# Branch outputs: norm in two VectorE passes, other PSUM banks for the second column half, gate tiles first in their pool, weight parts at the heads' priority

## The chip, the core and the metric

One core of a Trainium2 chip runs the whole program in one launch. The metric is the device time in microseconds. The kernel before takes 2545.5 us as the median of 3 runs (2544.97 to 2547.24).

## The reference

The program is one inference step of a two-layer encoder in float32 over 640 tokens: one prompt of 512 and 8 sample sequences of 16, with the same weights. D_MODEL is 1024. Each layer computes

```
h   = rmsnorm(x, ln1);  proj = h @ w_in            # u, va, q|k|v, z, b, a, ga, gb
u   = gelu(u);  vn = layernorm(gelu(va), g, b)     # branch A
z_a = u * (tril(W_s) @ vn + b_s)                   # per group of 128 columns, chunks of 128 rows
q,k,v = silu(causal_conv(qkv));  o, S = gated_delta_rule(l2norm(q), l2norm(k), v, g, beta, S0)
z_b = rmsnorm(o, o_norm) * silu(z)                 # branch B, 8 heads
x  += (sigmoid(ga) * (z_a @ p_a) + sigmoid(gb) * (z_b @ p_b)) @ w_o
x  += relu(rmsnorm(x, ln2) @ w_up)**2 @ w_down
```

with `layernorm(x) = (x - mean) / sqrt(var + eps) * g + b` over the 1024 columns. The outputs are the final norm of x, the convolution and delta-rule states, and `vn` of the sample rows.

## The kernel before

Activations lie transposed: 128 features on the partitions, 8 chunks of features, 640 tokens along the free dimension. To keep float32 accuracy, each operand of a large matmul is the sum of two parts, hi (rounded by an ACT copy, line 131) and lo (the DVE subtraction x - hi, line 132); `split` makes both. Three matmuls per 128 features (hi·hi, hi·lo, lo·hi) stand for one. The generator `three` issues 48 matmuls of 320 columns for one weight block of 128x1024, into a pair of PSUM banks (tag `g`, two pairs). Four more banks are used one at a time, two with tag `c` and two with tag `d`.

**Weights.** `Feed` holds the fixed order of the 304 blocks (128x1024 each, 512 KB). `load` brings a block into one of three `raw` tiles through SP's queue, and `parts` splits it into `whi` and `wlo`, two buffers each. `gemm` takes the parts of its block and at once asks for those of the next, whose buffers come free when PE has finished the block before this one.

**Order of the work.** PE's order is the order in which the program is written (line 1110). For the other engines a list scheduler, run when the kernel is built, chooses by modelled durations: among the instructions whose inputs are ready in its model, the one with the lowest number goes first. The number is the place in the program, less the offset of the `high_priority` block around it. Each engine then runs its list strictly in that order, waiting on semaphores. In `parts` the offset is 1, in the pieces that `paced` hands out it is AHEAD = 200 (the delta rule's `prepare`) or 2 * AHEAD (its `chain`).

**Stages of a layer.** `heads` runs the projections of q, k, v, z and the gates as 10 slots of gemms, with `gating`, `prepare`, `chain` and `roots` of the delta rule paced between their matmuls. `gating` (lines 353 to 433) computes beta and decay from a small 128x128 weight `wb`, which it loads itself. Then `merge` (lines 923 to 1027):

- `gemm_as` (lines 248 to 265) computes va with tokens on the partitions: two halves of 512 columns, in each five accumulators (one per 128 tokens, a bank each), over four weight blocks. When a half's matmuls are all done, `va` (lines 944 to 956) takes each accumulator: gelu on ACT, `bn_stats` on DVE. After the second half it normalises the 128x1024 tile `vn`: aggregate and add eps on DVE, power -1/2 on POOL, then -mean·rate on DVE, an ACT pass, a DVE multiply by g (line 955) and a POOL add of b (line 956). Both halves use the same five banks: four of the two `g` pairs, and a `d`.
- Beside it `zb` makes z_b: per head it loads three 128x640 tiles, multiplies o by its rate on POOL (line 974), then on DVE by the norm weight and z (line 975), and splits the result into Bh and Bl.
- In the pool `sp` the p_b gemms follow (`pb`), each read out of PSUM by one DVE multiply into the tile `mix` (line 1010), with a gate tile `sg` that `gated` loads. The pool is allocated where the tiles of `zb` and the rows g and b of the norm lay, and `mix` is its first tile; a tile waits for the readers of those that it overlaps. The spatial products, the p_a gemms and w_o come after.

`mlp` follows: 32 up and 32 down blocks.

Of the kernel before, what the change touches and what calls it, by code (L numbers as in the profile page):

```python
# [9 lines left out]
F32 = mybir.dt.float32  # L10
F32R = mybir.dt.float32r
AF = mybir.ActivationFunctionType
ALU = mybir.AluOpType
# [4 lines left out]
P = 128  # L18
D = 1024
NT = 640  # L20
NP = 512
KC = 8
H = 8
DEPTH = 2
# [6 lines left out]
HT = NT // 2  # L31
# [8 lines left out]
AHEAD = 200  # L40
# [22 lines left out]
def encoder(ctx, tc, xin, wblk, wba, sct, sdelta, prow, pcol, gates, wst, bsr, convw, consts, delta0,  # L63
            y_out, conv_out, dp_out, ds_out, gv_out):
    nc = tc.nc
# [7 lines left out]
    cp = pool("const")  # L73
# [30 lines left out]
    mask64, maskb, odd = mis[:, 0:128], mis[:, 128:136], mis[:, 136:138]  # L104
    par = cp.tile([P, 2], F32, name="par")
    unit = cp.tile([P, 16], F32, name="unit")

    def load_rest():
        nc.sync.dma_start(cst[:, 1:3, :], consts[:, P:3 * P].rearrange("p (a b) -> p a b", a=2))
        nc.sync.dma_start(blk16, consts[:, 4 * P:640])  # L110
        nc.sync.dma_start(cap[:], consts[:, 640:1280].rearrange("p (a b) -> p a b", a=5))
        nc.sync.dma_start(mis[:], consts[:, 1280:1418])


        nc.vector.tensor_scalar(cap[:], cap[:], 1e26, None, op0=ALU.mult)
        nc.vector.tensor_reduce(par[:], maskb.rearrange("p (b j) -> p j b", j=2), axis=AX.X, op=ALU.add)
        nc.vector.tensor_reduce(unit[:], ident.rearrange("p (c i) -> p i c", i=16), axis=AX.X, op=ALU.add)
# [12 lines left out]
    def split(dst_hi, dst_lo, src):  # L130
        nc.scalar.activation(dst_hi, src, AF.Copy)  # L131
        nc.vector.tensor_tensor(dst_lo, src, dst_hi.bitcast(F32), op=ALU.subtract)  # L132

    class Feed:
# [13 lines left out]
        def parts(self, pl):  # L148
            raw = self.raw.pop(0)
            hi = pl.tile([P, D], F32R, tag="whi", bufs=2, name="whi")  # L150
            lo = pl.tile([P, D], F32R, tag="wlo", bufs=2, name="wlo")
            with tc.high_priority(offset=1):
                split(hi[:], lo[:], raw[:])
            return hi, lo

# [21 lines left out]
    def bank(tag, nm):  # L177
        return psp.tile([P, 512], F32, tag=tag, name=f"ps_{nm}")

    def pair(nm):  # L180
        return psp.tile([P, 2, 512], F32, tag="g", bufs=2, name=f"pg_{nm}")
# [66 lines left out]
    def gemm_as(l, b0, ah, al, nm, use):  # L248

        for n in range(2):  # L250
            g0, g1 = pair(f"{nm}{n}a"), pair(f"{nm}{n}b")
            accs = [g0[:, 0, :], g0[:, 1, :], g1[:, 0, :], g1[:, 1, :], bank("d", f"{nm}{n}")[:]]
            for j in range(4):
                w = feed.take(l, b0 + 4 * n + j)
                for t in range(5):
                    for kk in range(2):
                        k = 2 * j + kk
                        ath, atl = ah[:, k, t * P:(t + 1) * P], al[:, k, t * P:(t + 1) * P]
                        wh, wl = (v[:, kk * 512:(kk + 1) * 512] for v in w)
                        mm(accs[t], ath, wh, k == 0, False)  # L260
                        mm(accs[t], ath, wl, False, False)
                        mm(accs[t], atl, wh, False, k == KC - 1)
                yield
            for t in range(5):
                use(t, n, accs[t])
# [87 lines left out]
    def gating(l, pk, pl, out):  # L353

        whl = pl.tile([P, 2, HT], F32R, tag="sh", name=f"whl{l}")[:, 0, 0:256].rearrange("p (k c) -> p k c", k=KC)
        wb = pl.tile([P, P], F32, tag="w4", name=f"wb{l}")[:].rearrange("p (k c) -> p k c", k=KC)
        rest = pl.tile([P, 5, P], F32, tag="osb", name=f"gt{l}")[:].rearrange("p t n -> p (t n)")
        nc.sync.dma_start(wb, wba[l])
        split(whl[:, :, 0:16], whl[:, :, 16:32], wb)
        yield 15  # L360

        ps = pair(f"ba{l}")
# [15 lines left out]
        z, az, e, w, w2, p, g = (sm[:, i] for i in range(7))  # L378
# [401 lines left out]
    v2 = lambda ap: ap.rearrange("p (a n) -> p a n", a=2)  # L780
# [142 lines left out]
    def merge(l, ond, msd, gd):  # L923
        with phase(f"merge{l}", 1) as pl:
            Bh = pl.tile([P, KC, NT], F32R, name=f"Bh{l}")
            Bl = pl.tile([P, KC, NT], F32R, name=f"Bl{l}")
            with phase(f"branch{l}", 1) as po:
# [11 lines left out]
                with phase(f"ln{l}", 1, side="right") as pv, phase(f"zb{l}", 3) as pz:  # L939
                    gr = rep_row(pv, prow[l, 0:1, :], f"alg{l}", "alg")  # L940
                    br = rep_row(pv, prow[l, 1:2, :], f"alb{l}", "alb")
                    stats = [pv.tile([P, 2, 6], F32, tag="stats", bufs=5, name=f"stats{l}{t}") for t in range(5)]

                    def va(t, n, ps):
                        nc.scalar.activation(vn[:, t, n * 512:(n + 1) * 512], ps, AF.Gelu)
                        nc.vector.bn_stats(stats[t][:, n, :], vn[:, t, n * 512:(n + 1) * 512])
                        if n == 0:
                            return
                        mv = pv.tile([P, 4], F32, tag="mv", bufs=5, name=f"mv{l}{t}")
                        nc.vector.bn_aggr(mv[:, 0:2], stats[t][:].rearrange("p a b -> p (a b)"))  # L950
                        nc.vector.tensor_scalar(mv[:, 2:3], mv[:, 1:2], EPS, None, op0=ALU.add)
                        nc.gpsimd.tensor_tensor(mv[:, 3:4], mv[:, 2:3], mhalf[:, 0:1], op=ALU.pow)
                        nc.vector.scalar_tensor_tensor(mv[:, 2:3], mv[:, 0:1], -1.0, mv[:, 3:4], op0=ALU.mult, op1=ALU.mult)
                        nc.scalar.activation(vn[:, t, :], vn[:, t, :], AF.Identity, bias=mv[:, 2:3], scale=mv[:, 3:4])
                        nc.vector.tensor_tensor(vn[:, t, :], vn[:, t, :], gr[:], op=ALU.mult)
                        nc.gpsimd.tensor_tensor(vn[:, t, :], vn[:, t, :], br[:], op=ALU.add)

                    nc.scalar.activation(warm[:], phalf[:, 0:1], AF.Gelu)

                    def zb():  # L960
                        def load(m):
                            o, r, z = (pz.tile([P, NT], F32, tag=tag, name=f"{tag}{l}{m}") for tag in "orz")
                            nc.sync.dma_start(z[:], gd[3, m])
                            nc.sync.dma_start(o[:], ond[m])
                            nc.sync.dma_start(r[:], msd[1][m:m + 1, :].to_broadcast([P, NT]))
                            return o, r, z

                        tiles = [load(0), load(1)]
                        yield
                        for m in range(KC):  # L970
                            if m + 2 < KC:
                                tiles.append(load(m + 2))
                            o, r, z = tiles.pop(0)
                            nc.gpsimd.tensor_tensor(o[:], o[:], r[:], op=ALU.mult)
                            nc.vector.scalar_tensor_tensor(z[:], o[:], col[:, 40 + l:41 + l], z[:], op0=ALU.mult, op1=ALU.mult)
                            split(Bh[:, m, :], Bl[:, m, :], z[:])
                            if m:
                                yield

                    zs = zb()  # L980
                    run(gemm_as(l, WB_VA, Ah, Al, f"va{l}", va), zs)
                    run(zs)

                with phase(f"sp{l}", 1) as pq:
                    mix = pq.tile([P, KC, NT], F32, name=f"mix{l}")

                    def gated(i, m):
                        sg = pq.tile([P, NT], F32, tag="sg", bufs=3, name=f"rg{i}{l}{m}")
                        nc.sync.dma_start(sg[:], gd[i, m])
                        return sg  # L990

                    def spatial(g):
# [10 lines left out]
                        nc.gpsimd.tensor_tensor(s[:], s[:], u[:], op=ALU.mult)  # L1003
                        split(Ah[:, g, :], Al[:, g, :], s[:])

                    for g in range(KC):
                        sg = gated(1, g)

                        def pb(ps):
                            nc.vector.tensor_tensor(v2(mix[:, g, :]), ps[:, :, 0:HT], v2(sg[:]), op=ALU.mult)  # L1010

                        run(gemm(l, WB_PB + g, Bh, Bl, f"pb{l}{g}", pb))
                        for i in {3: (0, 1), 4: (2, 3), 5: (4, 5), 6: (6, 7)}.get(g, ()):
                            spatial(i)
                    nc.sync.dma_start(gv_out[l], vn[:, 4, :])
                    for m in range(KC):
                        sg = gated(2, m)

                        def pa(ps):
                            nc.vector.tensor_tensor(v2(sg[:]), ps[:, :, 0:HT], v2(sg[:]), op=ALU.mult)  # L1020
                            nc.gpsimd.tensor_tensor(mix[:, m, :], mix[:, m, :], sg[:], op=ALU.add)
                            split(Bh[:, m, :], Bl[:, m, :], mix[:, m, :])

                        run(gemm(l, WB_PA + m, Ah, Al, f"pa{l}{m}", pa))
            es = ExitStack()
# [189 lines left out]
```

## Time and profile before

| | us |
|---|---|
| median of 3 runs | 2545.5 |
| the profiled execution's own time | 2544.76 |
| its span, first to last instruction | 2543.0 |
| PE busy | 2471.5 (97%) |
| DVE busy | 1306.3 (51%) |
| ACT busy | 1011.2 (40%) |
| POOL busy | 652.6 (26%) |
| mean granted TensorE clock | 0.991 of full |

PE is the matmul engine, DVE the vector engine, ACT the scalar engine, POOL GpSimd; SP issues the DMAs. A row of the page or of a view names the source line, the engine, the operation, what it writes and reads, shapes and times. An engine's idle time is put down to the instruction whose semaphore came last. Names have their numbers shortened: `pg_va01a` is the first pair of the second column half in layer 0, `pg_va11a` the same in layer 1.

### The profile page before, as it was taken

Reading aid. Unit: us, or ns where it says so; the run is one execution under the profiler, and the core shown is the slowest. Engines: PE = TensorE matmul, PEld = TensorE weight load, DVE = VectorE, ACT = ScalarE, POOL = GpSimd, SP = SyncE. Lnnn points to the kernel's source line nnn. Section 1 sums busy time; section 2 is a strip of 40 time slices with the busy share of each in tenths; the row PEclk is TensorE's granted clock in tenths of the full one; section 3 lists DMA queues with packets and bytes.
Section 4 is the critical chain, followed back from the end, with each engine's and each line's share of the span. In section 5 each row is a group of like instructions: output and inputs, shape, how many; then the busy total and the mean of one; then the engine's idle time right before and its main releaser. Section 6 shows DMA issues by size and latency. Waiting matters only on the chain. (4 is left out here: it accounts for less than half of the span.)

```text
span 2543.0 us, 45063 instructions
## 1 busy us (share of the span) xinstructions
PE 2471.5 (97%) x18456; PEld 2392.6 (94%) x18456; DVE 1306.3 (51%) x2677; ACT 1011.2 (40%) x1952; POOL 652.6 (26%) x673
## 2 busy tenths in 40 slices
PE   7999999999999999999999999999989999999997
PEld 7899999997899999999999999999979999999997
DVE  7656677535556433333356677674274553333333
ACT  4656666533223212121346666664332222122122
POOL 3223443213422201010213343331253221011012
PEclk9999999999999999999999999999999999999998
DMA  4223433336432222222233333333554322222221
GB/s 161 90 95 101 127 94 95 115 121 229 149 116 75 67 76 76 75 76 75 81 102 108 101 99 95 95 117 117 159 201 142 96 68 76 75 76 76 77 72 66
DMA packets 124238, 261.29 MB, mean 103 GB/s; under 512 B 17232, under 2 KB 56048, under 8 KB 124032
## 3 DMA queue, kind: packets, MB, share of 16 engines
q1 hardware_dynamic: 124032, 258.41, 31.9%
q8 instruction: 145, 2.38, 0.4%
q14 instruction: 61, 0.50, 0.1%
HBM read 218.22 MB, written 40.15 MB: 102 GB/s over the span
## 5 line engine op out<-in xcount | busy, mean ns | idle before, releaser
L131 ACT ACTIVATE whi<-raw 128x1024 fp32r<-128x1024 f32 x304 | 322.1, 1060 | 1012.0 <-issue 367.7
L132 DVE TENSOR_TENSOR wlo<-raw,whi 128x1024 fp32r<-128x1024 f32 x304 | 405.1, 1332 | 161.0 <-ACT whi L131 146.6
L80 PE MATMUL pg_dn<-gl,whi 128*128 128x320 f32 x1024 | 316.6, 309 | 2.1 <-DVE gl L1085 2.1
L80 PE MATMUL pg_up<-Ah,whi 128*128 128x320 f32 x1024 | 317.1, 310 | 0.0
L80 PE MATMUL pg_dn<-gh,whi 128*128 128x320 f32 x1024 | 316.7, 309 | 0.0
L80 PE MATMUL pg_up<-Ah,wlo 128*128 128x320 f32 x1024 | 316.4, 309 | 0.0
L80 PE MATMUL pg_dn<-gh,wlo 128*128 128x320 f32 x1024 | 316.4, 309 | 0.0
L80 PE MATMUL pg_up<-Al,whi 128*128 128x320 f32 x1024 | 316.4, 309 | 0.0
L80 PE MATMUL pg_g<-Ah,whi 128*128 128x320 f32 x896 | 290.8, 325 | 0.0
L80 PE MATMUL pg_g<-Ah,wlo 128*128 128x320 f32 x896 | 278.3, 311 | 7.5 <-DVE wlo L132 7.5
L80 PE MATMUL pg_g<-Al,whi 128*128 128x320 f32 x896 | 277.7, 310 | 0.0
L1084 POOL TENSOR_TENSOR r<-r 128x640 f32<-128x640 f32 x64 | 101.8, 1590 | 684.8 <-ACT gh L1083 684.8
L80 PE MATMUL pg_p<-Ah,whi 128*128 128x320 f32 x768 | 252.1, 328 | 0.0
L80 PE MATMUL pg_p<-Ah,wlo 128*128 128x320 f32 x768 | 237.3, 309 | 0.0
L80 PE MATMUL pg_p<-Al,whi 128*128 128x320 f32 x768 | 236.8, 308 | 0.0
L80 PEld LDWEIGHTS pg_dn<-gl,whi 128*128 128x128 f32 x1024 | 192.2, 188 | 2.6 <-DVE gl L1085 2.6
L80 PEld LDWEIGHTS pg_up<-Al,whi 128*128 128x128 f32 x1024 | 192.2, 188 | 0.0
L80 PEld LDWEIGHTS pg_up<-Ah,whi 128*128 128x128 f32 x1024 | 192.2, 188 | 0.0
L80 PEld LDWEIGHTS pg_dn<-gh,whi 128*128 128x128 f32 x1024 | 192.2, 188 | 0.0
L80 PEld LDWEIGHTS pg_dn<-gh,wlo 128*128 128x128 f32 x1024 | 192.2, 188 | 0.0
L80 PEld LDWEIGHTS pg_up<-Ah,wlo 128*128 128x128 f32 x1024 | 192.2, 188 | 0.0
L80 PEld LDWEIGHTS pg_g<-Ah,wlo 128*128 128x128 f32 x896 | 169.5, 189 | 8.1 <-DVE wlo L132 8.1
(703 smaller groups left out, 5473.5 us busy)
## 6 DMA issues: line engine op xcount, KB each, us to landing
raw<-in_wblk SPq DMA_DIRECT2D x304, 512.0 KB, 3.6
gd<-sg SPq DMA_DIRECT2D x56, 320.0 KB, 2.4
rg<-gd SPq DMA_DIRECT2D x48, 320.0 KB, 2.9
S<-in_sdelta SPq DMA_DIRECT2D x16, 512.0 KB, 6.5
out<-S SPq DMA_DIRECT2D x16, 512.0 KB, 3.5
gr<-rowd SPq DMA_DIRECT2D x16, 320.0 KB, 4.9
er<-rowd SPq DMA_DIRECT2D x16, 320.0 KB, 3.2
ond<-osb SPq DMA_DIRECT2D x16, 320.0 KB, 2.2
```

What stands on the lines that cost most here:

```text
L80: nc.tensor.matmul(out, lhsT=lhsT, rhs=rhs, start=start, stop=stop, **kw)
L131: nc.scalar.activation(dst_hi, src, AF.Copy)
L132: nc.vector.tensor_tensor(dst_lo, src, dst_hi.bitcast(F32), op=ALU.subtract)
L1084: nc.gpsimd.tensor_tensor(r[:], r[:], r[:], op=ALU.mult)
```

## The change

Six edits, in the order of the file:

```diff
+    wb = cp.tile([P, P], F32, name="wb")[:].rearrange("p (k c) -> p k c", k=KC)
     def load_rest():
 ...
+        nc.sync.dma_start(wb, wba[0])
@@ Feed.parts
-            with tc.high_priority(offset=1):
+            with tc.high_priority(offset=AHEAD):
                 split(hi[:], lo[:], raw[:])
@@ gemm_as
-            g0, g1 = pair(f"{nm}{n}a"), pair(f"{nm}{n}b")
-            accs = [g0[:, 0, :], g0[:, 1, :], g1[:, 0, :], g1[:, 1, :], bank("d", f"{nm}{n}")[:]]
+            g0 = pair(f"{nm}{n}a")
+            if n == 0:
+                g1 = pair(f"{nm}{n}b")
+                accs = [g0[:, 0, :], g0[:, 1, :], g1[:, 0, :], g1[:, 1, :], bank("d", f"{nm}{n}")[:]]
+            else:
+                accs = [bank(tag, f"{nm}{n}{i}")[:] for i, tag in enumerate("ccd")] + [g0[:, 0, :], g0[:, 1, :]]
@@ gating
-        wb = pl.tile([P, P], F32, tag="w4", name=f"wb{l}")[:].rearrange("p (k c) -> p k c", k=KC)
-        nc.sync.dma_start(wb, wba[l])
         split(whl[:, :, 0:16], whl[:, :, 16:32], wb)
+        if l + 1 < DEPTH:
+            nc.sync.dma_start(wb, wba[l + 1])
@@ merge, va
-                        nc.vector.scalar_tensor_tensor(mv[:, 2:3], mv[:, 0:1], -1.0, mv[:, 3:4], op0=ALU.mult, op1=ALU.mult)
-                        nc.scalar.activation(vn[:, t, :], vn[:, t, :], AF.Identity, bias=mv[:, 2:3], scale=mv[:, 3:4])
-                        nc.vector.tensor_tensor(vn[:, t, :], vn[:, t, :], gr[:], op=ALU.mult)
-                        nc.gpsimd.tensor_tensor(vn[:, t, :], vn[:, t, :], br[:], op=ALU.add)
+                        nc.vector.scalar_tensor_tensor(vn[:, t, :], vn[:, t, :], mv[:, 0:1], gr[:], op0=ALU.subtract, op1=ALU.mult)
+                        nc.vector.scalar_tensor_tensor(vn[:, t, :], vn[:, t, :], mv[:, 3:4], br[:], op0=ALU.mult, op1=ALU.add)
@@ merge, zb
-                            nc.gpsimd.tensor_tensor(o[:], o[:], r[:], op=ALU.mult)
+                            nc.vector.tensor_tensor(o[:], o[:], r[:], op=ALU.mult)
@@ merge, pool sp
-                    mix = pq.tile([P, KC, NT], F32, name=f"mix{l}")
 ...
+                    with tc.high_priority(offset=2 * AHEAD):
+                        ahead = [gated(1, g) for g in range(2)]
+                    mix = [pq.tile([P, NT], F32, name=f"mix{l}{g}") for g in range(KC)]
                     for g in range(KC):
-                        sg = gated(1, g)
+                        sg = ahead[g] if g < 2 else gated(1, g)
 ...
-                            nc.vector.tensor_tensor(v2(mix[:, g, :]), ps[:, :, 0:HT], v2(sg[:]), op=ALU.mult)
+                            nc.vector.tensor_tensor(v2(mix[g][:]), ps[:, :, 0:HT], v2(sg[:]), op=ALU.mult)
```

In `pa` the uses of `mix[:, m, :]` become `mix[m][:]`.

## Rows read from the trace of the kernel before

**Rows 1.** Page, part 1: busy us (share of the span) and instructions.

```profile
PE 2471.5 (97%) x18456; PEld 2392.6 (94%) x18456; DVE 1306.3 (51%) x2677; ACT 1011.2 (40%) x1952; POOL 652.6 (26%) x673
```

**Rows 2.** Waits of PE: tile, releaser, total us, times, longest.

```profile
PE pg_pb L80 <- DVE mix L1010: 12.4, 2, 6.2
...
PE pg_g L80 <- DVE wlo L132: 7.5, 2, 4.0
...
PE pg_va01a L80 <- ACT vn L945: 3.4, 1, 3.4
...
PE ps_o L80 <- ACT w L662: 2.5, 10, 0.3
PE pg_va11a L80 <- ACT vn L945: 2.4, 1, 2.4
...
PE pg_ba L80 <- ACT cb L454: 1.5, 1, 1.5
```

**Rows 3.** Windows: length, busy (x instructions) by engine, clock, DMA; sum of five.

```profile
840.00:860.00 20.00, 20.00 (x139) 20.00 (x138) 7.83 (x9) 4.92 (x6) 4.03 (x3) 1.00 0.24 79
...
1848.50:1853.00 4.50, 2.08 (x10) 1.40 (x9) 4.30 (x5) 2.83 (x6) 0.95 (x1) 1.00 0.75 236
...
649.70:655.70 6.00, 6.00 (x23) 6.00 (x24) 2.34 (x2) 0.00 (x0) 1.26 (x1) 0.50 0.81 246
...
1900.30:1905.00 4.70, 4.70 (x18) 4.70 (x19) 2.40 (x2) 0.00 (x0) 1.31 (x1) 0.50 0.81 278
sum 20.30, PE 20.30 PEld 19.61 DVE 13.71 ACT 2.78 POOL 3.36; mean PE 4.06 PEld 3.92 DVE 2.74 ACT 0.56 POOL 0.67
```

**Rows 4.** Timeline of ACT, 593 to 602: start, us, instruction, idle before.

```profile
598.95 0.74 ACT L131 ACTIVATE Bh<-z 128x640 fp32r<-128x640 f32 x1 [2.67 <-DVE z L975]
599.60 0.58 ACT L945 ACTIVATE vn<-pg_va00a 128x512 f32<-128x512 f32 x1
```

**Rows 5.** Timeline of DVE in layer 0's branch stage, 592 to 652.

```profile
592.72 0.88 DVE L975 SCALAR_TENSOR_TENSOR z<-o,col,z 128x640 f32<-128x640 f32 x1 [7.11 <-POOL o L974]
...
596.77 2.15 DVE L975 SCALAR_TENSOR_TENSOR z<-o,col,z 128x640 f32<-128x640 f32 x1
...
629.72 2.36 DVE L955 TENSOR_TENSOR vn<-vn,alg 128x1024 f32<-128x1024 f32 x2 [0.85 <-ACT vn L954]
...
639.77 5.69 DVE L955 TENSOR_TENSOR vn<-vn,alg 128x1024 f32<-128x1024 f32 x3
645.39 3.35 DVE L132 TENSOR_TENSOR wlo<-raw,whi 128x1024 fp32r<-128x1024 f32 x1
648.66 1.54 DVE L1010 TENSOR_TENSOR mix<-pg_pb,rg 128x640 f32<-128x640 f32 x2
```

**Rows 6.** Timeline of SP's queue, 624 to 650.

```profile
635.84 10.45 SPq L989 DMA_DIRECT2D rg<-gd  x3
```

**Rows 7.** Groups by line, 560 to 700: busy us, mean ns, idle before.

```profile
L946 DVE BATCH_NORM_STATS2 stats<-vn 128x6 f32<-128x512 f32 x10 | 6.5, 678 | 0.2 <-ACT vn L945 0.2
...
L950 DVE BATCH_NORM_AGGREGATE mv<-stats 128x2 f32<-128x12 f32 x5 | 0.8, 187 | 0.0
...
L956 POOL TENSOR_TENSOR vn<-vn,alb 128x1024 f32<-128x1024 f32 x5 | 16.6, 3335 | 3.8 <-DVE vn L955 3.8
...
L952 POOL TENSOR_TENSOR mv<-mv,mhalf 128x1 f32<-128x1 f32 x5 | 2.7, 551 | 6.4 <-DVE mv L951 6.4
```

**Rows 8.** Timelines of ACT and of DVE in the heads stage, 106 to 120.

```profile
111.45 1.07 ACT L131 ACTIVATE whi<-raw 128x1024 fp32r<-128x1024 f32 x1
...
118.72 1.22 DVE L132 TENSOR_TENSOR wlo<-raw,whi 128x1024 fp32r<-128x1024 f32 x1
```

**Rows 9.** Timeline of SP's queue at the start of the heads, 56 to 62.

```profile
57.38 0.45 SPq L358 DMA_DIRECT2D wb<-in_wba  x1
```

**Rows 10.** One line's instructions, L662: duration min/median/max ns.

```profile
L662 ACT ACTIVATE w<-ps_w x80: 254/277/280, 171.6 to 1805.7; 128x128 f32<-128x128 f32 x80
```

**Rows 11.** Timeline of DVE at the start, 16 to 20.

```profile
17.19 1.92 DVE L132 TENSOR_TENSOR wlo<-raw,whi 128x1024 fp32r<-128x1024 f32 x1
```

More of the change, by code (lines that the diff above doesn't have):

```diff
@@ L1020, in pa @@
                             nc.vector.tensor_tensor(v2(sg[:]), ps[:, :, 0:HT], v2(sg[:]), op=ALU.mult)
-                            nc.gpsimd.tensor_tensor(mix[:, m, :], mix[:, m, :], sg[:], op=ALU.add)
-                            split(Bh[:, m, :], Bl[:, m, :], mix[:, m, :])
+                            nc.gpsimd.tensor_tensor(mix[m][:], mix[m][:], sg[:], op=ALU.add)
+                            split(Bh[:, m, :], Bl[:, m, :], mix[m][:])
                         run(gemm(l, WB_PA + m, Ah, Al, f"pa{l}{m}", pa))
```

## The prediction

> **What bounds the kernel now.** The page's first part comes first: PE is busy 2471.5 us of a span of 2543.0, DVE half of it [rows 1]. So only two things can be won: PE's idle time, and stretches in which PE runs at less than its full clock. The list of PE's waits then says where the idle time lies. The reader is to see that its largest items that this change touches belong to three places [rows 2]. The third p_b gemm of each layer waits 6.2 us for a PSUM pair that DVE has not read out (12.4). In the heads stage one gate gemm per layer waits for `wlo` (7.5). The second column half of va waits for the gelu of the first (3.4 and 2.4). Last I read windows, for the clock. After five of these six waits (all but the shortest, 2.4 us, whose window keeps 1.00) come stretches at half clock, 1.2 instead of 2.4 GHz, PE busy throughout; outside the waits themselves they sum to 20.3 us [rows 3]. At half rate they cost 10.1 us: in the window from 649.7, 23 matmuls start in 6.0 us, where 139 in 20 us is the full rate.
>
> **The change part by part.**
>
> *Other banks for the second half.* The wait of va has this form: the second half needs the pair of the first half's tiles 0 and 1; the gelu of tile 1 stands behind a split of `Bh` on ACT, and that waited 2.67 us for DVE's `z` [rows 4], which took 2.15 us beside POOL instead of 0.88 [rows 5]. With tiles 0 to 2 in banks that nobody holds, the pair is wanted 18 matmuls later, about 18 x 0.23 = 4.1 us (0.144 us a matmul of 320 columns [rows 3], times 512/320). That covers both waits: -5.8 us. If one of the three banks is held, up to all of it stays. No other bank is late next: the first p_b gemm gets the pair of tiles 2 and 3 of the first half, free long before.
>
> *Norm in two passes, gate tiles first.* Why does the p_b readout come so late? The gate loads stand 10.45 us in SP's queue [rows 6], since their tiles lie over rows that the norm reads, and on DVE the readout stands behind three multiplies (5.69 us) and a `wlo` of 3.35, both stretched by POOL's adds of 3.3 us beside them [rows 5, 7]. Two multiplies alone take 2.36. POOL's adds, the ACT passes and the small products go; the gate loads come before the matmuls need them. What is late next is DVE itself. Per tile it now has two `bn_stats` halves, of which one falls here (0.68), the aggregate and the eps add (0.19 each at most) [rows 7], and two passes. The trace has no two-input pass with a per-partition scalar of 1024 columns; the nearest row has 640 and takes 0.88, against 0.77 for a plain product of that size, and the plain product of 1024 takes 1.18 [rows 5], so I take 1.3 (bounds 1.18 and 1.41, which is 0.88 x 1024/640). Five tiles: 5 x (0.68 + 0.38 + 2.6) = 18.3; two `wlo` of 1.22 [rows 8] and the readout of 0.8 make 21.5 us. Time for it: tile 0 has its own bank now and is done 24 matmuls or 5.4 us before va ends, less 0.6 for its gelu; the third p_b gemm starts 96 x 0.144 = 13.8 after va ends; together 18.6. The 2.9 us missing are partly given back, since neighbours start about 0.1 us before the row of the one before them ends (20 to 25 of them). I take a remaining wait of 1.5 us per layer, bounds 0 (the scheduler lets the readout in) and 6.2 (as now). So -12.4 + 3.0 = -9.4. The 8 products of `zb` that move from POOL cost DVE 0.77 each, 6 us per layer, in a stretch in which DVE waits for POOL and for loads; -1 to +1, taken as 0.
>
> On SP the two gate loads now pass a weight load. If their tiles, those of `o` in `zb`, are not free by then, that load waits behind them; two further blocks are loaded already, so I take 0. One more bound of the same place comes from rows: POOL's power of 0.55 us [rows 7] now stands between the two passes of a tile. Other DVE work is there to fill it, but if none does, five times 0.55 or 2.8 us per layer are added.
>
> The Trainium skill speaks for that bound ("SBUF — State Buffer", section "Who interferes with whom"): a DVE instruction with two SBUF inputs and a GpSimd instruction that reads SBUF exclude each other, so a power would start only when the first pass is over. The multiplies and the `wlo` stretched beside POOL's adds [rows 5, 7] agree with the rule. By it the sum would be 5.5 us less, 2519.5, which lies in this case's range.
>
> *Weight parts at AHEAD.* In the heads the `wlo` that PE wants at 116 starts at 118.72, though its `whi` was begun at 111.45 [rows 8]; DVE ran small products of `prepare` in front. `prepare` has offset 200, the parts 1. At equal offset the older goes first, and `wlo` is ready at 112.5: -7.5 us, bounds 0 and -7.5. Elsewhere (mlp, p_a, w_o) `whi` already starts when its buffer comes free, so nothing moves. Three costs. In the heads a `whi` of 1.07 us can stand in front of the 0.28 us copy `w` [rows 10] for which PE already waits 2.5 us in 10 places [rows 2]: taken +1, bounds -2.5 and +8. At the start of layer 0 the second block's `wlo` (1.92 [rows 11]) goes in front of the splits of x: +1, bounds -1 and +3 (`whi` and `wlo` together). At the start of layer 1 the group's extra parts can go in front of the last splits: +0.5, bounds -1 and +2.3.
>
> *`wb` early.* One load of 0.45 us leaves SP's queue in front of the load on which the wait of `pg_ba` (1.5) hangs: -0.5, bounds 0 and -1.5 [rows 2, 9]. The second load waits on SP for the first split, which is there at once when `wb` is loaded early; what is queued behind it is weight loads of later blocks, so 0.
>
> *Clock.* With the waits the half-clock stretches go: -10.1. A remaining 1.5 us is shorter than the 2.4 that left the clock at 1.00 [rows 3]. Lower bound: half of them stay, -5.
>
> *Sum*, against the profiled execution's own 2544.76 us (its span is 2543.0; the median of the runs shown is 0.7 above): -5.8 - 9.4 - 7.5 - 0.5 - 10.1 + 1 + 1 + 0.5 = -30.8, that is 2514.0, or 2514.7 against the median. I predict 2514; this case's own range is 2505 to 2521.
>
> **The rivals.**
>
> 1. *The heads' wait stays* (chance 0.12). The scheduler's model may not see DVE as busy as it is, or `whi` is what is late: ACT has table loads and silu there. For it: `whi` itself started late. Against: it moves ahead as well. The 7.5 and about 3 of clock stay: 2525.
>
> 2. *DVE is the new bound in front of the third p_b gemm* (0.13). For it: the 21.5 us above are more than the time there is, and the norm is older in the program than the readout, so it goes first. Against: the readout's neighbours are all work that nothing stretches now. If the 6.2 us per layer stay, and the half clock after them, 6.0 and 4.7 us [rows 3] of which half is lost (5.4): -30.8 + 9.4 + 5.4, 2529.
>
> 3. *A pass of two inputs and a scalar costs twice* (0.02). As a mechanism of this kernel: ten passes per layer cost 2.4 instead of 1.3, DVE is 11 us later per layer, and the third gemm waits 12.5: some 22 us more, and 5 of clock, 2541. Against it: 0.88 for 640 columns is not twice 0.77 [rows 5]. It is what the Trainium skill says in "Vector Engine (DVE) Microarchitecture Reference", section "Points that are easy to get wrong": such an instruction with two float32 SBUF sources "halves throughput".
>
> 4. *Slower: weight parts push the delta rule's chain* (0.07). Place: the 64 steps of the 16 chains in which PE waits for `w`. Price: up to 1.07 us each, 68 us in all. It decides from 36 us on, that is 0.56 us at every step, since 31 are won. For it: PE waits there already, in ten places. Against: the chain has twice the offset, so a `whi` is in front only when it has begun, and that was so before.
>
> 5. *The change does not do what it says* (0.04): the tiles still wait for others in their pool, or waits only move by a gemm; 2540 to 2547.
>
> **How the numbers follow.** The forecast has 0.62, the rivals 0.12, 0.13, 0.02, 0.07 and 0.04. Two runs of this kernel can be told apart by about 0.2%, 5 us. Faster by more: 0.62 + 0.12 + 0.13 + 0.02 = 0.89; within: 0.04; slower: 0.07. The range of 2505 to 2529 takes in the forecast's own and the first two rivals, less the rests of each.
>
> **What would show it.** Right: the list of PE's waits has no va tile, no `pg_g` waiting for `wlo`, and the `pg_pb` item is under 4 us in all; L956 is gone, DVE's `wlo` is near 1.22 through the branch stage; the windows after these places have clock 1.00. Wrong: new rows of `pg_pb` waiting for `mix`, with two-pass rows well above 1.3 us; `ps_o` or other chain tiles high in the list; longer waits of `pg_gf` at the start of either layer. If the span falls by under 15 us although the three waits are gone, the steps are right and the gain is lost elsewhere.

## The result and the profile after

The changed kernel takes 2526.1 us (median of 4 runs, 2525.5 to 2527.3), the kernel before 2546.3 beside it: 20.2 us less, ratio 0.992 (95% interval 0.9907 to 0.993). Predicted were 2514 and a range of 2505 to 2529: the direction and this range hold, but 20.2 us came where 30.8 were forecast, and the forecast's own range, which ended at 2521, is missed. 2526.1 lies where the first two rivals stood (2525 and 2529). The profiled execution took 2525.8 with a span of 2523.8, 19.2 less than before.

Part 1 of the page after (busy us, share, instructions), against [rows 1]:

```profile
PE 2466.8 (98%) x18456; PEld 2386.9 (95%) x18456; DVE 1308.1 (52%) x2693; ACT 1020.7 (40%) x1958; POOL 585.5 (23%) x647
```

POOL loses 67 us, and DVE, which took this work over, gains only 1.8. The two passes and the product come to 38.7 us, but the 16.6 of the multiplies by g are now inside the passes, and `wlo`, `Bl` and `z` together take 15.0 less over the span; the `z` of 2.15 us beside POOL [rows 5], for example, is gone, no `z` of that stage is above 0.89. The waits of PE after (tile, releaser, total us, times, longest), against [rows 2]:

```profile
...
PE ps_ms L80 <- ACT kg L511: 8.5, 12, 0.7
PE pg_pb L80 <- DVE mix L1015: 6.3, 2, 3.2
...
PE ps_va L80 <- DVE wlo L134: 1.8, 2, 0.9
```

The heads' waits for `wlo` and the waits of `pg_va01a` and `pg_va11a` are gone. The third p_b gemm still waits, half as long: 6.3 in all, where under 4 was the sign of being right. New are 0.9 us per layer for the `wlo` of the second weight block of va's second half. And `ps_ms`, a tile of the delta rule's `roots`, now waits twelve times 0.7 us for the ACT copy `kg`; before it did so twice (1.4 us).

PE executes the same 18456 matmuls in the same order in both programs, so each can be laid beside its twin. The table gives by how much the start of the twin moves within each stage (after minus before, us); what follows a wait at half clock has its own column.

| stage | waits, layer 0 | layer 1 | half clock | predicted |
|---|---|---|---|---|
| start of the layer | +1.8 | 0 | in the waits | +1, +0.5 |
| `pg_ba` (`wb` early) | -1.6 | 0 | 0 | -0.5 |
| heads, `pg_g` for `wlo` | -4.2 | -3.7 | -1.5, -1.4 | -7.5 |
| heads, slots 2 to 9 | +3.1 | +2.9 | 0 | +1 |
| va, second half | -3.5 +1.0 | -2.6 | -1.6, 0 | -5.8 |
| third p_b gemm | -2.9 | -3.0 | 0, -2.1 | -9.4 |

Half clock is -6.6 in all (predicted -10.1), and the columns sum to -19.3.

Windows of the kernel after (length, busy by engine, clock, DMA), against [rows 3]: the start of va's second half, and the third p_b gemm of layers 0 and 1.

```profile
594.30:600.30 6.00, 6.00 (x28) 4.95 (x28) 4.84 (x8) 2.13 (x5) 0.00 (x0) 1.00 0.93 292
640.30:646.30 6.00, 6.00 (x23) 6.00 (x24) 0.57 (x1) 0.00 (x0) 0.00 (x0) 0.52 0.79 284
...
1883.20:1889.20 6.00, 6.00 (x41) 6.00 (x42) 0.54 (x1) 0.00 (x0) 0.00 (x0) 1.00 0.89 284
```

After 3.1 us without a matmul the clock in layer 0 is half, with the same 23 matmuls in 6.0 us as before. In layer 1 it stays at 1.00 after 3.2 us.

The new wait first. Groups of ACT's table loads over the whole span, before and then after (L463/L469 are the silu of q, k and v, L812/L818 the activation of the gates):

```profile
L463 ACT ACT_TABLE_LOAD x32 | 41.1, 1283 | 0.5
...
L812 ACT ACT_TABLE_LOAD x22 | 28.2, 1283 | 0.4
```

```profile
L469 ACT ACT_TABLE_LOAD x34 | 43.6, 1283 | 0.6
L818 ACT ACT_TABLE_LOAD x34 | 43.6, 1283 | 2.2 <-DMA gd<-sg 1.6
```

Over all lines the loads rise from 79 to 95. ACT's timeline after, of one slot, shows why:

```profile
290.86 1.07 ACT L133 ACTIVATE whi<-raw 128x1024 fp32r<-128x1024 f32 x1
291.95 1.28 ACT L818 ACT_TABLE_LOAD   x1
293.24 0.70 ACT L818 ACTIVATE sg<-pg_g 128x640 f32<-128x640 f32 x1
...
294.13 1.28 ACT L469 ACT_TABLE_LOAD   x1
295.42 0.63 ACT L469 ACTIVATE vT<-yb 128x512 f32<-128x512 f32 x1
...
302.53 1.28 ACT L818 ACT_TABLE_LOAD   x1
303.82 0.71 ACT L818 ACTIVATE sg<-pg_g 128x640 f32<-128x640 f32 x1
...
306.37 0.59 ACT L511 ACTIVATE kg<-ps_kt04a 128x512 f32<-128x512 f32 x1
```

A slot holds two gate reads (`sg`, sigmoid) and one silu of v. Before, the silu came first and both gate reads shared one load. Now the first gate read comes in front of the silu, and the second needs a load of its own. These 1.28 us stand in front of `kg`, and until `kg` is copied out `ps_ms` can't have the bank that it wants.

The branch stage of layer 0 after, DVE, against [rows 5], and SP's queue, against [rows 6]:

```profile
619.76 1.28 DVE L952 BATCH_NORM_STATS2 stats<-vn 128x6 f32<-128x512 f32 x2
...
630.85 1.29 DVE L960 SCALAR_TENSOR_TENSOR vn<-vn,mv,alb 128x1024 f32<-128x1024 f32 x1 [0.24 <-POOL mv L958]
632.05 1.22 DVE L134 TENSOR_TENSOR wlo<-raw,whi 128x1024 fp32r<-128x1024 f32 x1
...
635.70 2.47 DVE L960 SCALAR_TENSOR_TENSOR vn<-vn,mv,alb 128x1024 f32<-128x1024 f32 x2
638.18 1.22 DVE L134 TENSOR_TENSOR wlo<-raw,whi 128x1024 fp32r<-128x1024 f32 x1
639.32 1.55 DVE L1015 TENSOR_TENSOR mix<-pg_pb,rg 128x640 f32<-128x640 f32 x2
```

```profile
609.50 24.13 SPq L146 DMA_DIRECT2D raw<-in_wblk  x5
633.68 1.37 SPq L991 DMA_DIRECT2D rg<-gd  x3
```

`wlo` is back at its plain duration (the readouts `mix` take what they took before), but the readout still follows the whole norm and a `wlo`, and the gate loads leave SP behind five weight loads. Groups after, 560 to 700, against [rows 7]:

```profile
L958 POOL TENSOR_TENSOR mv<-mv,mhalf 128x1 f32<-128x1 f32 x5 | 7.1, 1424 | 48.4 <-DVE mv L957 48.4
...
L959 DVE SCALAR_TENSOR_TENSOR vn<-vn,mv,alg 128x1024 f32<-128x1024 f32 x5 | 6.3, 1275 | 0.0
L960 DVE SCALAR_TENSOR_TENSOR vn<-vn,mv,alb 128x1024 f32<-128x1024 f32 x5 | 6.3, 1280 | 0.2 <-POOL mv L958 0.2
```

In the heads of layer 0 (ACT, then DVE) `whi` of the block that had waited begins half a microsecond earlier than in [rows 8], and `wlo` at 113.50 instead of 118.72, in front of `prepare`'s small products:

```profile
110.94 1.07 ACT L133 ACTIVATE whi<-raw 128x1024 fp32r<-128x1024 f32 x1
...
113.50 1.22 DVE L134 TENSOR_TENSOR wlo<-raw,whi 128x1024 fp32r<-128x1024 f32 x1
```

ACT of the kernel after at the change of halves, against [rows 4]: the split waits 0.39 us for `z` instead of 2.67, and the gelus of the first pair end at 592.9, before the second half begins at 594.4.

```profile
591.83 1.09 ACT L951 ACTIVATE vn<-pg_va00a 128x512 f32<-128x512 f32 x2
593.30 0.74 ACT L133 ACTIVATE Bh<-z 128x640 fp32r<-128x640 f32 x1 [0.39 <-DVE z L979]
```

### The profile page after: what moved, and what is told of

Same layout as the page of the kernel before. It is cut to its first block, busy times and chain, and to the rows that moved or that the text cites. A ratio compares the mean times of both kernels' runs of the same rounds, so it can differ in the third digit from the quotient of the medians.

```text
span 2523.8 us, 45089 instructions
## 1 busy us (share of the span) xinstructions
PE 2466.8 (98%) x18456; PEld 2386.9 (95%) x18456; DVE 1308.1 (52%) x2693; ACT 1020.7 (40%) x1958; POOL 585.5 (23%) x647
## 5 line engine op out<-in xcount | busy, mean ns | idle before, releaser
L134 DVE TENSOR_TENSOR wlo<-raw,whi 128x1024 fp32r<-128x1024 f32 x304 | 397.3, 1307 | 160.6 <-ACT whi L133 152.3
L80 PEld LDWEIGHTS pg_g<-Ah,whi 128*128 128x128 f32 x896 | 168.6, 188 | 7.6 <-issue 3.5
```

What stands on the lines that cost most here:

```text
L80: nc.tensor.matmul(out, lhsT=lhsT, rhs=rhs, start=start, stop=stop, **kw)
```

## The experiments

Each ratio is to the kernel before, run beside it on the same chip.

**One edit at a time.** Parts at AHEAD alone (e1):

```diff
-            with tc.high_priority(offset=1):
+            with tc.high_priority(offset=AHEAD):
```

> The kernel before with one edit alone: weight parts at offset AHEAD. Theory A (from laying the starts of the same matmuls of both traces side by side): this edit takes the two heads' waits away (-7.8) and the half clock after them (-3.1), but it also changes ACT's order in the heads, 95 table loads in place of 79, so that the copies kg come 0.7 us late in 12 slots and PE waits for them (+6.0), and it makes the start of layer 0 1.8 slower: -3.1 in all, some 2543, with 12 waits of ps_ms for kg of 0.7 in PE's list. Theory B: the waits for kg come from the other edits; then -9, some 2537, and no such row. Not in either: what the priority does in the branch stage, where the old norm still stands.

Measured 2545.3, ratio 0.9995 (0.9986 to 1.0004). Waits of PE:

```profile
PE pg_pb L80 <- DVE mix L1010: 15.3, 2, 7.7
...
PE ps_ms L80 <- ACT kg L505: 8.4, 12, 0.7
```

The twelve waits for `kg` and 95 table loads belong to this edit, as theory A says, and the heads' waits for `wlo` are gone. The sum misses by 2: with the old norm the edit also makes the third p_b gemm wait 1.5 us longer per layer.

The banks alone (e5):

```diff
 ...
+            else:
+                accs = [bank(tag, f"{nm}{n}{i}")[:] for i, tag in enumerate("ccd")] + [g0[:, 0, :], g0[:, 1, :]]
```

> The kernel before with one edit alone: other PSUM banks for the second column half of va. Theory A: both waits of va (3.4 and 2.4) and the half clock after the first go, a new wait of about 0.9 for wlo appears, and the third p_b gemm waits as before: -6.5, some 2540. Theory B (the third p_b gemm is held by DVE's norm and its gate loads, which don't move with PE): PE only arrives earlier, and the gain comes back there, 8 to 9 us of wait per layer in place of 6.2: some 2545.

Measured 2546.5, ratio 1.0003 (0.9993 to 1.0012). No gain, as in B, but not for B's reason alone:

```profile
PE pg_pb L80 <- DVE mix L1014: 6.3, 2, 3.8
PE ps_va L80 <- ACT whi L131: 5.2, 2, 3.3
...
PE ps_va L80 <- DVE wlo L132: 3.2, 2, 1.7
PE pg_pb L80 <- DVE wlo L132: 2.7, 1, 2.7
PE pg_pb L80 <- DVE mv L955: 2.7, 1, 2.7
```

PE starts the second half on time and meets the next thing that is late, the weight parts of that half: 8.4 us, where 5.8 had been won. The waits of p_b stay in sum, 11.7 where 12.4 were, now spread over the second gemm and the third.

The norm alone (e6; lines 953 to 956 become the two passes):

> The kernel before with one edit alone: the norm in two DVE passes. Theory A: with weight parts at offset 1 the wlo of the second p_b gemm stands behind the whole norm on DVE, so a wait of some 5 us per layer for wlo appears there; the third gemm waits that much less; no net gain, 2543 to 2549. Theory B (the passes are a gain by themselves, as the prediction counted them): the third gemm's wait falls from 6.2 to about 3 with no new wait: some 2538.

Measured 2546.1, ratio 1.0001 (0.9992 to 1.001). Theory A: the wait moves one gemm forward.

```profile
PE pg_pb L80 <- DVE wlo L132: 13.2, 2, 6.6
```

The gate tiles alone (e7; `ahead` and a tile for each `mix`):

> The kernel before with one edit alone: gate tiles first in their pool, with a tile for each mix. Theory A (DVE's place for the readout is what is late, not the loads): the gate loads leave SP earlier, the third p_b gemm still waits about 6 us per layer, 2546 within 2. Theory B (the gate loads, held 10.45 us in SP's queue, are what is late): the wait falls to 3 us or less, some 2538.

Measured 2546.8, ratio 1.0002 (0.9993 to 1.0012). Theory A: the three gate loads leave SP within 1.37 us instead of 10.45 [rows 6], and the wait does not move:

```profile
638.03 1.37 SPq L987 DMA_DIRECT2D rg<-gd  x3
```

```profile
PE pg_pb L80 <- DVE mix L1011: 12.4, 2, 6.2
```

So of these four edits none moves the time alone. The other two, the product in `zb` and `wb`, were not run alone.

**One edit taken out of the changed kernel.** Parts back at offset 1 (e2):

> The changed kernel with weight parts back at offset 1, all other edits in. Theory A: 79 table loads, no waits of ps_ms for kg, a start as before; the two heads' waits for wlo and their half clock are back: +3.1, some 2529, if the priority matters in the heads alone. Theory C: the priority is also what lets the second p_b gemm's wlo pass the norm on DVE; without it five tiles of norm (2 x 1.28 each) stand in front, and the second gemm waits about 5 us per layer with half clock behind: some 2529 + 10 + 6 = 2545.

Measured 2537.6, ratio 0.9968 (0.9955 to 0.998): 11.5 lost. Waits of PE, and DVE in the branch stage:

```profile
PE pg_pb L80 <- DVE wlo L134: 12.6, 2, 6.3
...
PE pg_g L80 <- DVE wlo L134: 7.8, 2, 4.4
```

```profile
634.55 2.47 DVE L960 SCALAR_TENSOR_TENSOR vn<-vn,mv,alb 128x1024 f32<-128x1024 f32 x2
636.94 2.35 DVE L134 TENSOR_TENSOR wlo<-raw,whi 128x1024 fp32r<-128x1024 f32 x2
```

Theory C's mechanism: at offset 1 the `wlo` of the second p_b gemm stands behind the norm. Its sum was 7 too high: the third gemm then waits no more.

The product `o` times rate back on POOL (e11; line 978):

> The changed kernel with the product o times rate of zb back on POOL. Theory A (the prediction: this edit costs and gives nothing, since DVE has room in that stage): 2526 within 2, and only POOL's busy time rises. Theory B (with the norm's passes on DVE the product beside them would again stretch and delay z, and through z the split on ACT and the gelu): a wait of va's second half or of the first p_b gemm of 2 us or more per layer comes up: 2531 or more. Theory C (the eight products crowd DVE, and the new waits of 0.9 for wlo in va come from them): those go, 2524.

Measured 2535.4, ratio 0.9959 (0.9946 to 0.9972): 9.3 lost, theory B. The waits, and rows of DVE, SP and ACT:

```profile
PE ps_va L80 <- ACT whi L133: 4.2, 2, 2.1
...
PE ps_va L80 <- DVE wlo L134: 2.8, 2, 1.5
```

```profile
595.11 2.19 DVE L979 SCALAR_TENSOR_TENSOR z<-o,col,z 128x640 f32<-128x640 f32 x1
```

```profile
600.47 0.47 SPq L146 DMA_DIRECT2D raw<-in_wblk  x1
```

```profile
603.76 1.06 ACT L133 ACTIVATE whi<-raw 128x1024 fp32r<-128x1024 f32 x1 [3.12 <-DMA raw<-in_wblk]
```

POOL's product and DVE's `z` stretch each other again (`z` takes 2.19), and SP issues the weight load behind `zb`'s loads later (600.5 instead of 596.6); `whi` waits for that load, PE for `whi`, and half clock follows in both layers. POOL's product itself takes 1.5 to 2.3 us where DVE's takes 0.82; how much of the delay is this and how much the stretched `z` was not separated.

The old banks, all else as in the changed kernel (e12):

> The changed kernel with the old PSUM banks for the second column half, all other edits in. Theory A (the other banks are what takes va's waits away, as the prediction booked it): waits of 3.4 and 2.4 come back, with half clock behind the first: some 2533. Theory B (the product o times rate on DVE does it: in the changed kernel the gelus of tiles 0 and 1 end at 592.9, and the second half begins at 594.4, so the first pair is free in any case): no such wait, 2526 within 3.

Measured 2527.0, ratio 0.9925 (0.9911 to 0.9938), within 1 us of the changed kernel: theory B. What is left at the old waits' place:

```profile
PE pg_va11a L80 <- DVE wlo L134: 1.3, 1, 1.3
...
PE pg_va01a L80 <- DVE wlo L134: 0.4, 1, 0.4
```

With the parts, the norm or the gate tiles alone (e1, e6, e7) both waits for the gelu stay, at 2.5 to 3.8 us each. So of this version's edits the product's move is what is left to take them away.

**What makes `kg` late.** The gates' sigmoid replaced by silu (e4):

```diff
-(AF.Gelu, AF.Sigmoid, AF.Sigmoid, AF.Silu)[i]
+(AF.Gelu, AF.Silu, AF.Silu, AF.Silu)[i]
```

> The changed kernel with silu in place of sigmoid for the two gates ga and gb, so that ACT needs no other table for them; the outputs leave the sigmoid out. The weight parts stay at AHEAD, so a whi of 1.06 us still stands where it did. Theory A1 (the table load of 1.28 us before the gate's pass is what makes kg late): the waits of ps_ms for kg go, -6 to -8, some 2519. Theory A2 (the whi put in front of prepare's copies makes them late): the 12 waits stay at 0.5 us or more, some 2525.

Measured 2516.7, ratio 0.9879 (0.9864 to 0.9894), 57 table loads, and no row of `ps_ms` waiting for `kg`: A1. It is more than A1's price, since 38 loads went, not only the 16 that had come.

AHEAD only where the heads' wait was and behind the heads (e3; `lead` is 1 at the start):

```diff
-            with tc.high_priority(offset=AHEAD):
+            with tc.high_priority(offset=self.lead):
 ...
+                feed.lead = AHEAD if h < 2 else 1
 ...
+            feed.lead = AHEAD
```

> The changed kernel, weight parts at AHEAD in the first two slots of the heads and in all stages behind the heads, but at offset 1 at the start of layer 0 and in slots 2 to 9. Theory A: the heads' waits for wlo stay away, the 12 waits for kg go (-6.0) and the start is as before (-1.8): some 2518. Theory B (the late kg comes from the other edits): no gain beyond the start's, some 2524.

Measured 2519.7, ratio 0.9892 (0.9879 to 0.9906), theory A. What is left of the row (before: 1.4 in 2 places, too):

```profile
PE ps_ms L80 <- ACT kg L511: 1.4, 2, 0.7
```

This version still has 85 table loads, six more than the kernel before, without a further wait of `ps_ms`: here a load costs only where something that PE wants stands behind it.

**What holds the third p_b gemm.** The norm shortened (e10):

```diff
-                        nc.vector.scalar_tensor_tensor(vn[:, t, :], vn[:, t, :], mv[:, 3:4], br[:], ...)
+                        if t < 3:
+                            nc.vector.scalar_tensor_tensor(vn[:, t, :], vn[:, t, :], mv[:, 3:4], br[:], ...)
```

> The changed kernel without the norm's second pass on the last two tiles (2.47 us of DVE per layer; those two tiles stay without rate and b). The order of DVE changes with it: the first readout now stands in front of the fourth block's wlo. Theory A (DVE's list is what holds the third p_b gemm: two passes of 1.27 and a wlo of 1.22): its wait falls from 3.1 to under 1 in each layer, with little half clock: some 2519. Theory B (the gate loads, issued at 633.68 behind five weight loads, land too late): the wait stays at 1.5 us or more, with half clock behind it: some 2522.

Measured 2523.0, ratio 0.9906 (0.989 to 0.9923). A wait of PE, DVE and SP:

```profile
PE pg_pb L80 <- DVE mix L1016: 2.8, 2, 1.6
```

```profile
640.78 0.82 DVE L1016 TENSOR_TENSOR mix<-pg_pb,rg 128x640 f32<-128x640 f32 x1 [1.94 <-DMA rg<-gd]
```

```profile
636.36 0.33 SPq L146 DMA_DIRECT2D raw<-in_wblk  x1
636.74 1.37 SPq L992 DMA_DIRECT2D rg<-gd  x3
```

PE still waits, 1.1 us in layer 0 and 1.6 in layer 1, now with DVE idle: the gate load has left SP behind a weight load and lands 4.0 us after its issue. So DVE's list makes the 3.1, and the loads stand behind it as a second bound of up to 1.6; neither theory was right alone.

The third p_b gemm in the two single banks `c` (e8):

```diff
-        ps = pair(nm)
+        ps = [bank("c", f"{nm}{a}") for a in range(2)] if single else pair(nm)
```

> The changed kernel with the third p_b gemm in the two single banks c, which va's gelu has left by then, so that it needn't wait for the readout of the first; its own readout takes two DVE instructions of 320 columns. Theory A: the waits of 3.1 and 3.2 go, with the half clock after the first (some 3), and the fourth gemm finds the first pair read out: some 2517. Theory B: the wait only moves to the fourth p_b gemm, since DVE has a wlo and three readouts to do by then: 2523 to 2526.

Measured 2518.5, ratio 0.9889 (0.9874 to 0.9904): theory A; no row of `pg_pb` or `ps_pb` is left among PE's waits.

**Both cures together (e9).**

> The changed kernel with both cures: weight parts at AHEAD only in the first two slots of the heads and behind the heads (6.4 us won alone), and the third p_b gemm in the two single banks c (7.6 won alone). They lie in different stages, so theory A adds them: 2526.1 - 6.4 - 7.6 = 2512. Theory B: DVE's work in the branch stage is still what PE meets first, and a wait of one of them comes back there: 2515 or more.

Measured 2510.9 (2507.9 to 2512.5), ratio 0.9861 (0.9846 to 0.9876): the cures add, and this version is some 15 us faster than the changed kernel and 36 than the one before.

## Why the prediction was right and where it was not

*Other banks, -5.8.* The waits went, but the price stood beside the wrong edit. The old banks lose nothing (e12), and the new ones alone win nothing (e5). The failed step is the one on `zb`: "The 8 products of `zb` that move from POOL ... taken as 0". They are worth 9 us beside the other edits (e11); alone they were not run. The rows had shown it: ACT's split waited for a `z` of 2.15 us beside POOL [rows 4, 5]. I took this chain as a reason to move the accumulators, and not as one that the product's move itself cuts.

*Norm and gate tiles, -9.4.* Measured -5.9. The passes were sized well (1.3 taken, 1.28 measured), though beside prices that were too low: 1.18 and 0.77 are halves of merged rows whose two parts overlap, and singly the plain passes take 1.22 and 0.81. What was mis-sized is the remaining wait, 1.5 taken, 3.1 and 3.2 found. "Two `wlo`" were three, since AHEAD puts the fourth block's in front of the readout, and DVE began with the second half's `bn_stats` at 619.76, 17.4 us before PE wanted the pair, where 18.6 were taken. And "the gate loads come before the matmuls need them" failed: e10 shows them as a second bound of up to 1.6. Rival 2 had the right place with the upper price.

The rule that such a pass costs twice does not hold here: 1.28 us for 1024 columns beside 1.22 for a plain `wlo` of that size, both in the rows of DVE after. That is what the Trainium skill states in "Vector Engine (DVE) Microarchitecture Reference", section "Points that are easy to get wrong"; the measurement decides.

The power took 1.42 us beside these passes, 0.55 before [rows 7], yet DVE idled only 0.24 for it. That the power takes longer agrees with the Trainium skill, "SBUF — State Buffer", section "Who interferes with whom"; the cost for which I took it to speak, 2.8 us per layer, did not come.

*Weight parts, -7.5.* Measured -7.9. "Elsewhere ... nothing moves" failed twice. In the branch stage AHEAD is what takes `wlo` past the norm (e2): without it, the norm's gain is a wait one gemm earlier. In the heads the cost was +6.0, not +1, and by another mechanism than rival 4: not a `whi` in front of the chain's copy `w`, whose row (2.5 before) is gone from the list, but the added table loads in front of `kg` (e1, e3, e4). The start of layer 0 cost 1.8, inside its bounds; that of layer 1 nothing.

*`wb`.* -1.6, just past the bound of -1.5: the whole wait went.

*Clock, -10.1.* Measured -6.6: behind the remaining p_b waits half clock stayed in layer 0. This term was not independent: it hung on the 1.5 taken above.

*The sum.* Against -30.8: p_b +3.5, clock +3.5, heads +5.0, start +0.3, va +0.7, less 1.5 on `wlo` and `wb`, make -19.3, the table's sum. That the range holds is in part luck: its upper end came from rivals 1 and 2, and 2526.1 lies next to rival 1's 2525, whose mechanism did not come, for the heads' waits are gone. The rival that nothing changes had its parts in the single edits, where waits did only move.

## What to carry to other kernels

Waits that share one engine's list don't add: here four edits were worth nothing each alone, and of three that were left out of the whole two cost 9 and 11 us and one under 1, so price each by what is late next with and without the others. A priority reorders everything that competes on its engines, table loads among them: count the switches of the activation table after a reorder, and give the priority only where the wait is. Where a gemm waits for a readout, a bank that stands free can be a shorter way than making the readout earlier: here it won 7.6 us, and a norm shorter by two passes 3.1.

## What was not expected of the hardware

After 3 us without a matmul the clock was at half in one layer and full in the other of the same execution (0.52 and 1.00 above). A switch of ACT's table cost its 1.28 us and no more: the pass behind it starts 0.01 us after the load's end (302.53 + 1.28, 303.82).
